# Reordering the top-16 search of two token tiles in a hybrid decoder step, with a different row cadence

## The chip, the cores and the metric

The kernel runs on one core of one Trainium2 chip. The metric is the device time of one execution in microseconds (us); of several runs the median is given. A smaller time is better. Five engines work side by side, each through its own instruction list in order: PE (TensorE, matrix products; its weight loads are shown apart as PEld), DVE (VectorE), ACT (ScalarE), POOL (GpSimd) and SP (SyncE, which only issues transfers here). They meet through semaphores, and 16 DMA engines move the data.

## The reference

One decoder layer is computed for 256 prompt tokens and 8 sample tokens that share all weights (D = 2048, everything float32):

```python
proj = x @ w_in
y_a = ssd_branch(...);  y_b = shortconv_branch(...)
mix = sigmoid(g_a) * (y_a @ w_branch_ssd) + sigmoid(g_b) * (y_b @ w_branch_sc)
x1 = layer_norm(ALPHA * x + mix @ w_out)
x2 = layer_norm(ALPHA * x1 + peer(x1))
y  = x2 + sigmoid(x2 @ ple_gate_w) * (p @ ple_proj_w)

def peer(x):                       # 8 heads, 16384 experts of one neuron each
    q = x @ w_q                    # per head two halves of 128
    t1, i1 = top_k(q[..., 0] @ keys1.T, 16);  t2, i2 = top_k(q[..., 1] @ keys2.T, 16)
    top, pos = top_k(all 256 sums t1 + t2, 16)
    idx = the expert numbers i1 * 128 + i2 at pos;  gate = softmax(top)
    hid = gelu(x . u_tab[idx]);  return sum over experts of gate * hid * v_tab[idx]
```

The change concerns `peer`, from the search over the scores to the products with the experts' rows.

## The kernel before

**Two ways to the experts.** For the first 208 prompt tokens (TD) the kernel works densely: it multiplies all 16384 experts' `u` rows with the tokens (the *u stage*: 128 blocks, one `pair_block` each), multiplies the result with a table of gates that is zero wherever an expert was not chosen, and multiplies that with all `v` rows (the *v stage*: 8 groups c of 16 blocks). The other 48 prompt tokens and the 8 samples (NSP = 56) are worked sparsely: for each of 56 columns a *row gather* (`get`, L1297, an indirect DMA on POOL's queue) brings 128 chosen rows of `uR`, 1 MB, and one DVE product over 128x2048 uses them; then the same with `vR`. That makes 112 row products, in three groups of 32, 16 and 8 columns, `u` before `v` in each (`sparse_experts`, L1289).

**What PE needs.** Every float32 weight is split into a rounded high part and the rest. A weight block of 1 MB is loaded by SP (L146) as two halves of 1024 columns; per half ACT writes `whi` (L158), DVE writes `wlo` (L159). Five pairs of `whi`/`wlo` exist in the u and v stages, so the split runs at most five halves ahead. A dense block is 15 + 1 products of 416 columns with `whi` (L293, the last one is L296) and 16 of 208 columns with `wlo` (L294).

**What sets the order.** The program is written out by Python, and the order on each engine is the order in which the code issues. After each half block `tick` raises a counter and lets background tasks (generators) issue work: each tick gives them a credit of 1.1 in these stages, and a yield of a number takes that credit, which stands for the DVE's time in us. A yield of ("w", n) waits n ticks. A task at the head of the list goes first. `Grid` keeps a task at a fixed step of ticks. Where the code needs a task's result before it can go on (`run_out`, or the loop after the u stage that waits for the last gates), it ticks with no block in between: then PE gets no instruction at that place.

**The selection.** `TT` names three tiles: tile 0 = tokens 128 to 255, tile 1 = the samples (64 rows, one per sample and head), tile 2 = tokens 0 to 127. `head_topk(h)` takes a head's scores; `topk` (L1095 to L1100, five DVE operations) finds the 16 best of 128 for one tile and one half. When all eight heads are done for all tiles, `select_all` runs `select` for tile 0, 1 and 2 in turn. `send` writes the sparse tokens' indices and gates to memory. `gates` (L1260) builds, four tokens per 3 ticks, the one-hot factors on POOL, DVE and ACT, `g_mm` multiplies them on PE (L1286), and a block of 32 tokens goes out to the table `g_d` (2 MB, L1278). Tokens 128 to 207 (20 steps) come after tile 0's selection, tokens 0 to 127 (32 steps) after tile 2's.

**The turn from u to v.** When the last gates are out, `to_v` gives the selection's memory to the v stage's buffers (`vp`), starts `residual` (16 ACT copies into `acc`, L1503) and `prep(0)`: four pieces k, each loading gates `gl` and hidden values `al` (L1430, L1431, L1433, two buffers each, on POOL's queue), multiplying them on DVE (L1446, L1447) and splitting the result into `co` (L1457 on ACT, L1458 on DVE). All four pieces must have been issued before the first block of v is (`run_out`).

Of the kernel before, what the change touches and what calls it, by code (L numbers as in the profile page):

```python
# [10 lines left out]
F = mybir.dt.float32  # L11
# [12 lines left out]
TD = T - NSP  # L24
# [6 lines left out]
PH = 8  # L31
# [12 lines left out]
STEP = 4  # L44
# [7 lines left out]
def hybrid_step(ctx: ExitStack, tc: tile.TileContext, xT, pT, w_in, w_dt, w_bs, w_bc, w_o, w_q, w_pg, w_pp,  # L52
# [111 lines left out]
    tasks = []  # L164
    later = []
    clock = {"t": 0, "credit": 0.0, "in": False}
# [892 lines left out]
    TT = ((PT // 2, 128, PH), (PT, 64, 1), (0, 128, PH))  # L1059
# [5 lines left out]
    t2_stack = ExitStack()  # L1065
# [36 lines left out]
    def head_topk(h):  # L1102
        load_keys(h)
        yield ("w", 2)
        for s in range(2):
            ac.copy(zq[:, s, h, 8 * h:8 * h + 8], Q[2 * h + s][:, PT:T])
        yield ("w", 1)
        k = keys_sb.pop(h)
        ps2 = {}
        for t in (0, 2):  # L1110
            t0, n, _ = TT[t]
            ps = bank("scr")
            for s in range(2):
                te.matmul(ps[:n, s * 128:(s + 1) * 128], Q[2 * h + s][:, t0:t0 + n], k[:, s], start=True, stop=True)
            v = t2.tile([128, 2, 128], F, name="sv", tag="sv", bufs=3)
            ac.copy(v[:n].rearrange("p s k -> p (s k)"), ps[:n, 0:256])
            ps2[t] = v
            yield 0.1
        if h == 0:
            SC["ps"] = bank("scp")  # L1120
        for s in range(2):
            te.matmul(SC["ps"][:64, s * 128:(s + 1) * 128], zq[:, s, h], k[:, s],
                      start=(h == 0 and s == 0), stop=(h == PH - 1), skip_group_check=True)
        if h == PH - 1:
            v = t2.tile([128, 2, 128], F, name="sv", tag="sv", bufs=3)
            ac.copy(v[:64].rearrange("p s k -> p (s k)"), SC.pop("ps")[:64, 0:256])
            ps2[1] = v
        for t, v in sorted(ps2.items()):
            n = TT[t][1]
            for s in range(2):  # L1130
                hh = h if t != 1 else 0
                topk(v[:n, s], TV[t][s][:n, hh], TI[t][s][:n, hh], n)
                yield 1.1
        Q.pop(2 * h)
        Q.pop(2 * h + 1)
        DONE[h] = True

    def select(t, sel):

# [66 lines left out]
    def select_all():  # L1206
        while sum(h in DONE for h in range(PH)) < PH:
            yield ("w", 1)
        t2_stack.close()
        sp = P["sp"] = sp_stack.enter_context(tc.tile_pool(name="select", bufs=1))  # L1210
        P["oh"] = oh_stack.enter_context(tc.tile_pool(name="onehot", bufs=1))
        for t, (t0, n, nh) in enumerate(TT):
            sel = sp.tile([128, 3, nh * TOPK], F, name=f"sel{t}")
            yield from select(t, sel)
            if t < 2:
                send(sel, t, nh)
            if t == 1:
                spawn(sparse_experts(), True)
            if t != 1:
                nd = min(n, TD - t0)  # L1220
                yield ("w", 2)
                ps = bank("slt")
                for q in range(3):
                    te.transpose(ps[:, q * 128:q * 128 + n], sel[:n, q], ident[:n, :n])
                for q in range(3):
                    ac.copy(slot[q][:, t0:t0 + nd], ps[:, q * 128:q * 128 + nd])
                if t == 0:
                    tasks.insert(0, {"gen": gates(t0, nd), "wait": clock["t"] + 1})
        while "G" + str(PT // 2) not in DONE:
            yield ("w", 1)  # L1230
        yield from gates(0, PT // 2)
# [57 lines left out]
    def sparse_experts():  # L1289
# [64 lines left out]
        for i, (tab, k0, n, c) in enumerate(jobs):  # L1354
            ks = slice(k0, k0 + n)
            if tab is uR and c == k0:
                x1s = XR.pop(g)
            if tab is vR and c == k0 and g + 1 < len(GR):
                while g + 1 == len(GR) - 1 and "sent" not in DONE:
                    yield ("w", 1)  # L1360
                index(g + 1)
                spawn(replicate(g + 1))
            get(i + 1)
            yield grid(STEP - (i % (4 if vp else 2) == 0))
            t = rows.pop(i)
            if tab is uR:
                ve.scalar_tensor_tensor(t, t, 1.0, x1s, OP.mult, OP.mult, accum_out=shid[:, c:c + 1])  # L1367
                yield 2.4
                if c == k0 + n - 1:
                    yield ("w", 1)  # L1370
                    ac.activation(shid[:, ks], shid[:, ks], AF.Gelu)
                    ve.tensor_tensor(scf[:, ks], shid[:, ks], scf[:, ks], OP.mult)
                continue
            if c == k0:
                ve.tensor_scalar(x1s, t, scf[:, c:c + 1], None, OP.mult)
            else:
                ve.scalar_tensor_tensor(x1s, t, scf[:, c:c + 1], x1s, OP.mult, OP.add)  # L1377
            yield 2.4
            if c == k0 + n - 1:
                spawn(folded(g, x1s), True)  # L1380
                g += 1
# [318 lines left out]
```

## Time and profile before

| | |
|---|---|
| median of 3 runs | 2459.51 us (2458.3 to 2460.56) |
| the profiled execution, its own time | 2465.26 us |
| its span, first to last instruction | 2463.5 us |
| mean granted PE clock over the span | 0.997 |
| last matmul of the first and of the last u block (L296) starts at | 1057.5 and 1738.5 us |
| the same of the v stage | 1743.1 and 2351.2 us |
| first and last row product (L1367, L1377) | 1250.5 and 2296.1 us |
| last copy-out of one-hot gates issued (L1278) | 1641.84 us |

Times inside the trace are microseconds from the start of the span. A row of the table of windows gives the length of the window and each engine's busy time in it with its number of instructions, then the granted PE clock (1.00 is full), the share of the 16 DMA engines' time that was in use, and GB/s. A row of the waits gives the engine and line that waited, what it waited for, the total, how often, and the longest. A row of the timeline or of a chain gives start, duration, engine, line, operation and tiles, and in square brackets the idle time of the engine ahead of it with what ended it.

### The profile page before, as it was taken

The numbers are of one execution on the slowest core, as the hardware profiler recorded it, in microseconds if no ns is written. First come the engines' busy times: TensorE is split into PE (matmuls) and PEld (weight loads), VectorE is DVE, ScalarE is ACT, GpSimd is POOL, SyncE is SP. The second block draws the span as 40 slices with busy tenths as digits, with TensorE's granted clock in tenths as the row PEclk, the third lists the DMA queues.
The fourth block names the chain that finished last, engine by engine and source line by source line (L and its number), as shares of the span: only waits on it lengthen the run. The fifth ranks groups of instructions, "written<-read, shape, count | busy, mean of one in ns | idle before, by whom it ended". The sixth has DMA issues, their size and how long they took to land.

```text
span 2463.5 us, 47946 instructions
## 1 busy us (share of the span) xinstructions
PE 2418.6 (98%) x19049; PEld 2394.8 (97%) x19049; DVE 2008.5 (82%) x3192; ACT 1458.7 (59%) x2310; POOL 620.0 (25%) x720
## 2 busy tenths in 40 slices
PE   9999999999999999999999999999999999999989
PEld 9999999999999999998999999999999999999988
DVE  8788886566455578999998777779999989989987
ACT  6776664554444455654777878866544555444564
POOL 2232221000000010100346667632332223322210
PEclk9999999999999999999999999999999999999999
DMA  6687786555555555566779999999999999999654
GB/s 247 229 289 260 261 265 204 193 189 202 191 202 191 193 201 189 196 212 203 238 291 347 358 359 372 368 352 396 399 374 382 382 375 392 376 374 371 223 190 147
DMA packets 137104, 688.90 MB, mean 280 GB/s; under 512 B 15744, under 2 KB 53168, under 8 KB 63280
## 3 DMA queue, kind: packets, MB, share of 16 engines
q1 hardware_dynamic: 89168, 495.46, 56.3%
q0 software_dynamic: 28688, 158.69, 16.7%
q10 hardware_dynamic: 19024, 31.69, 3.5%
q8 instruction: 149, 2.44, 0.4%
q14 instruction: 75, 0.61, 0.1%
HBM read 646.32 MB, written 39.46 MB: 278 GB/s over the span
## 4 chain that ended last, share of the span: by engine, by line
PE 63%; DVE 15%; DMA 11%; ACT 5%; issue 5%; ACTq 0%; POOL 0%; DVEq 0%; SPq 0%; POOLq 0%
PE mm L255 14%; PE mm L257 14%; PE mm L256 14%; PE mm L293 11%; DVE wlo L159 7%; PE mm L294 6%; DMA w<-vP 5%; DMA w<-uT 4%; ACT whi L158 2%; DVE ug L1367 1%; PE gps L1286 1%; ACT o L1274 1%; PE mm L296 1%; DMA a_d<-as 1%; DMA g_d<-gs 1%
## 5 line engine op out<-in xcount | busy, mean ns | idle before, releaser
L159 DVE TENSOR_TENSOR wlo<-w,whi 128x1024 fp32r<-128x1024 f32 x916 | 1112.0, 1223 | 333.9 <-ACT whi L158 328.0
L158 ACT CAST whi<-w 128x1024 fp32r<-128x1024 f32 x916 | 943.1, 1044 | 629.8 <-DMA w<-vP 247.0
L293 PE MATMUL mm<-x,whi 128*128 128x416 f32 x1920 | 572.7, 365 | 4.1 <-ACT whi L158 4.1
L293 PE MATMUL mm<-co,whi 128*128 128x416 f32 x1920 | 561.8, 361 | 0.0
L255 PE MATMUL mm<-x,whi 128*128 128x264 f32 x1920 | 532.4, 277 | 0.0
L257 PE MATMUL mm<-x,wlo 128*128 128x264 f32 x1920 | 530.2, 276 | 0.5 <-DVE wlo L159 0.4
L256 PE MATMUL mm<-x,whi 128*128 128x264 f32 x1920 | 529.9, 276 | 0.0
L294 PE MATMUL mm<-x,wlo 128*128 128x208 f32 x2048 | 504.7, 257 | 16.2 <-DVE wlo L159 15.9
L294 PE MATMUL mm<-co,wlo 128*128 128x208 f32 x2048 | 500.8, 255 | 7.2 <-DVE wlo L159 7.2
L294 PEld LDWEIGHTS mm<-x,wlo 128*128 128x128 f32 x2048 | 392.8, 193 | 25.0 <-DVE wlo L159 24.4
L294 PEld LDWEIGHTS mm<-co,wlo 128*128 128x128 f32 x2048 | 390.7, 192 | 11.5 <-DVE wlo L159 11.4
L293 PEld LDWEIGHTS mm<-x,whi 128*128 128x128 f32 x1920 | 365.6, 190 | 5.8 <-ACT whi L158 4.6
L255 PEld LDWEIGHTS mm<-x,whi 128*128 128x128 f32 x1920 | 362.9, 189 | 1.4 <-issue 1.4
L257 PEld LDWEIGHTS mm<-x,wlo 128*128 128x128 f32 x1920 | 362.9, 189 | 1.1 <-DVE wlo L159 1.1
L293 PEld LDWEIGHTS mm<-co,whi 128*128 128x128 f32 x1920 | 363.3, 189 | 0.0
L256 PEld LDWEIGHTS mm<-x,whi 128*128 128x128 f32 x1920 | 362.9, 189 | 0.0
L1273 POOL TENSOR_SCALAR o<-iot,slot,slot 128x128 f32<-128x128 f32 x156 | 191.1, 1232 | 2.7 <-issue 0.9
L1297 POOL DMA_INDIRECT ug<-vR,sidx x56 | 106.9, 1908 | 270.4 <-DVE x1s L1377 228.8
L1297 POOL DMA_INDIRECT ug<-uR,sidx x56 | 93.0, 1660 | 264.2 <-DVE ug L1367 204.8
L1367 DVE SCALAR_TENSOR_TENSOR ug<-ug,x1s 128x2048 f32<-128x2048 f32 x56 | 127.8, 2282 | 2.2 <-DMA ug<-uR,sidx 2.2
L1377 DVE SCALAR_TENSOR_TENSOR x1s<-ug,scf,x1s 128x2048 f32<-128x2048 f32 x53 | 124.4, 2347 | 0.4 <-DMA ug<-vR,sidx 0.4
L893 POOL CAST r1h<-r1gbh 128x2 fp32r<-128x2 f32 x16 | 7.5, 468 | 439.9 <-DVE mxl L242 439.9
(364 smaller groups left out, 3939.9 us busy)
## 6 DMA issues: line engine op xcount, KB each, us to landing
w<-uT SPq DMA_DIRECT2D x128, 1024.0 KB
w<-vP SPq DMA_DIRECT2D x128, 1024.0 KB
w<-w_in SPq DMA_DIRECT2D x118, 1024.0 KB
w<-w_bc SPq DMA_DIRECT2D x16, 1024.0 KB
w<-w_bs SPq DMA_DIRECT2D x16, 1024.0 KB
w<-w_o SPq DMA_DIRECT2D x16, 1024.0 KB
w<-w_q SPq DMA_DIRECT2D x16, 1024.0 KB
w<-w_pg SPq DMA_DIRECT2D x16, 1024.0 KB
```

The costliest lines, as they stand in the source:

```text
L158: ac.copy(hi, w)
L159: ve.tensor_tensor(lo, w, hi.bitcast(F), OP.subtract)
L255: te.matmul(ps, wh, vh, start=(first and q == 0), stop=False)
L256: te.matmul(ps, wh, vl, start=False, stop=False)
L257: te.matmul(ps, wl, vh, start=False, stop=(last and q == n - 1))
L293: te.matmul(ps, hi[:, ws], both, start=(kb == 0), stop=False)
L294: te.matmul(ps[:, :TD], lo[:, ws], one, start=False, stop=False)
L296: te.matmul(ps, hi[:, ws], both, start=False, stop=True)
L1273: (gp if q < 3 else ve).tensor_scalar(o1[:, q], iot, slot[0][:, c], slot[2][:, c], OP.is_equal, OP.mult)
L1297: gp.indirect_dma_start(out=t, out_offset=None, in_=tab, in_offset=bass.IndirectOffsetOnAxis(ap=sidx[:, c:c + 1], axis=0))
L1367: ve.scalar_tensor_tensor(t, t, 1.0, x1s, OP.mult, OP.mult, accum_out=shid[:, c:c + 1])
L1377: ve.scalar_tensor_tensor(x1s, t, scf[:, c:c + 1], x1s, OP.mult, OP.add)
```

## The change

Four things are altered. The second-stage score tiles `sv` of tile 2 get eight buffers of their own and are kept. `head_topk` searches only tile 0 and, at the last head, the samples; tile 2's 16 searches are done in `select_all`, after tile 0's selection. `sparse_experts` is started after tile 0's selection instead of after the samples', and the one-hot gates of tokens 128 to 207 start after tile 2's searches. The row products' cadence goes from 3 and 4 ticks in turn to 3, 4, 4, 4 in the u stage, and from 3, 4, 4, 4 to 4 throughout in the v stage (`vp` is set from the turn on).

```diff
         for t in (0, 2):
...
-            v = t2.tile([128, 2, 128], F, name="sv", tag="sv", bufs=3)
+            v = t2.tile([128, 2, 128], F, name="sv", tag="sv" + str(t), bufs=2 if t == 0 else PH)
...
+        late_sv.append(ps2.pop(2))
         for t, v in sorted(ps2.items()):
-            n = TT[t][1]
-            for s in range(2):
-                hh = h if t != 1 else 0
-                topk(v[:n, s], TV[t][s][:n, hh], TI[t][s][:n, hh], n)
-                yield 1.1
+            yield from tile_topk(t, v, h if t != 1 else 0)
...
+    late_sv = []
+
+    def tile_topk(t, v, h):
+        n = TT[t][1]
+        for s in range(2):
+            topk(v[:n, s], TV[t][s][:n, h], TI[t][s][:n, h], n)
+            yield 1.1
...
-        t2_stack.close()
         sp = P["sp"] = sp_stack.enter_context(tc.tile_pool(name="select", bufs=1))
-        P["oh"] = oh_stack.enter_context(tc.tile_pool(name="onehot", bufs=1))
         for t, (t0, n, nh) in enumerate(TT):
+            if t == 1:
+                for h, v in enumerate(late_sv):
+                    yield from tile_topk(2, v, h)
+                t2_stack.close()
+                P["oh"] = oh_stack.enter_context(tc.tile_pool(name="onehot", bufs=1))
+                tasks.insert(0, {"gen": gates(TT[0][0], TD - TT[0][0]), "wait": clock["t"] + 1})
             sel = sp.tile([128, 3, nh * TOPK], F, name=f"sel{t}")
             yield from select(t, sel)
             if t < 2:
                 send(sel, t, nh)
-            if t == 1:
+            if t == 0:
                 spawn(sparse_experts(), True)
...
-                if t == 0:
-                    tasks.insert(0, {"gen": gates(t0, nd), "wait": clock["t"] + 1})
...
-            yield grid(STEP - (i % (4 if vp else 2) == 0))
+            yield grid(STEP - (not vp and i % 4 == 0))
```

Two places show how the lists move. The first is DVE's list where the row products begin. In the kernel before, the first one (L1367, on tile `ug`) stands among the last selection's operations (`big`, `sel`) and the one-hot factors (`o_`), after 35 of the 128 u blocks (an `as` row closes a block):

```order
L1192 TENSOR_TENSOR big<-big,idf 128x512
L159 TENSOR_TENSOR wlo_13259<-w,whi_13258 128x1024
L1367 SCALAR_TENSOR_TENSOR ug,shid<-ug,x1s 128x2048
L159 TENSOR_TENSOR wlo_97<-w,whi_93 128x1024
L1412 TENSOR_TENSOR as<-mm,as 128x208
L159 TENSOR_TENSOR wlo_95<-w,whi_92 128x1024
L1273 TENSOR_SCALAR o_15422<-iot,slot_13263,slot_13265 128x128
L1194 TENSOR_REDUCE sel_14971<-big 128x32
```

In the changed kernel it stands after 24 blocks, among tile 2's searches (`tv`, `ti`, `sw`):

```order
L159 TENSOR_TENSOR wlo_95<-w,whi_92 128x1024
L1419 TENSOR_TENSOR as<-mm,as 128x208
L1374 SCALAR_TENSOR_TENSOR ug,shid<-ug,x1s 128x2048
L159 TENSOR_TENSOR wlo_96<-w,whi_91 128x1024
L159 TENSOR_TENSOR wlo_94<-w,whi_90 128x1024
L1419 TENSOR_TENSOR as<-mm,as 128x208
L1095 MAX tv_12040<-sv 128x8
L1096 MAX_INDEX ti_12046<-tv_12040,sv 128x8
L1098 MATCH_REPLACE sw<-tv_12040,sv 128x128
L1099 MAX tv_12040<-sw 128x8
L1100 MAX_INDEX ti_12046<-tv_12040,sw 128x8
L159 TENSOR_TENSOR wlo_13271<-w,whi_13270 128x1024
```

What moved: the row products now come with the searches of tile 2, and 25 of them (11 before) stand ahead of the end of tile 2's selection, which falls in block 70 (54 before).

The second place is DVE's list at the end of the u stage. In the kernel before, the last blocks of u (`as` rows) and the first of v (`acc`) stand next to each other, with only weight splits and row products between, since all four pieces of `co` were issued blocks earlier:

```order
L1377 SCALAR_TENSOR_TENSOR x1s<-ug,scf,x1s 128x2048
L159 TENSOR_TENSOR wlo_13259<-w,whi_13258 128x1024
L1412 TENSOR_TENSOR as<-mm,as 128x208
L159 TENSOR_TENSOR wlo_97<-w,whi_93 128x1024
L159 TENSOR_TENSOR wlo_95<-w,whi_92 128x1024
L1482 SCALAR_TENSOR_TENSOR acc<-acc,mm 128x416
L159 TENSOR_TENSOR wlo_96<-w,whi_91 128x1024
```

In the changed kernel three of the four pieces (`al<-al,gl`, then `co<-al,co`) stand behind the last `as` row, with row products in between and no weight split:

```order
L1419 TENSOR_TENSOR as<-mm,as 128x208
L1453 TENSOR_TENSOR al<-al,gl 128x4x192
L1454 TENSOR_TENSOR al<-al,gl 128x4x16
L1465 TENSOR_TENSOR co<-al,co 128x8x104
L1384 SCALAR_TENSOR_TENSOR x1s<-ug,scf,x1s 128x2048
L1453 TENSOR_TENSOR al<-al,gl 128x4x192
L1454 TENSOR_TENSOR al<-al,gl 128x4x16
L1465 TENSOR_TENSOR co<-al,co 128x8x104
L1384 SCALAR_TENSOR_TENSOR x1s<-ug,scf,x1s 128x2048
L1453 TENSOR_TENSOR al<-al,gl 128x4x192
L1454 TENSOR_TENSOR al<-al,gl 128x4x16
L1465 TENSOR_TENSOR co<-al,co 128x8x104
```

What moved: the last one-hot step stands after 119 u blocks instead of 105, `to_v` runs when 5 blocks of u are left instead of 19, and the preparation of the first v group goes past the end of u. Counted in ticks (two a block), 17 ticks lie between the last u block and the first v block, in which PE is given no dense block; before there are none. By the first v block 60 row products stand ahead (53 before), and the last of the 112 stands at half 209 of the 256 of v (232 before).

More of the change, by code (lines that the diff above doesn't have):

```diff
@@ L1124, in head_topk @@
         if h == PH - 1:
-            v = t2.tile([128, 2, 128], F, name="sv", tag="sv", bufs=3)
+            v = t2.tile([128, 2, 128], F, name="sv", tag="sv0", bufs=2)
             ac.copy(v[:64].rearrange("p s k -> p (s k)"), SC.pop("ps")[:64, 0:256])
             ps2[1] = v
+        late_sv.append(ps2.pop(2))
         for t, v in sorted(ps2.items()):
-            n = TT[t][1]
-            for s in range(2):
-                hh = h if t != 1 else 0
-                topk(v[:n, s], TV[t][s][:n, hh], TI[t][s][:n, hh], n)
-                yield 1.1
+            yield from tile_topk(t, v, h if t != 1 else 0)
         Q.pop(2 * h)
```

## The prediction

> **What bounds the kernel now.** First the page: which engine fills the span.
>
> ```profile
> span 2463.5 us, 47946 instructions
> PE 2418.6 (98%) x19049; PEld 2394.8 (97%) x19049; DVE 2008.5 (82%) x3192; ACT 1458.7 (59%) x2310; POOL 620.0 (25%) x720
> ```
>
> PE is busy 98% of the span, and its work does not change, so only its idle time can move. The windows say where that lies (length; busy PE, PEld, DVE, ACT, POOL; clock; DMA share; GB/s).
>
> ```profile
> core 0: us, PE busy (x) PEld busy (x) DVE busy (x) ACT busy (x) POOL busy (x), PEclk, DMA share, GB/s
> ...
> 1057.00:1142.00 85.00, 85.00 (x594) 83.36 (x594) 81.75 (x273) 45.36 (x76) 1.61 (x3) 1.00 0.66 220
> 1142.00:1260.00 118.00, 108.56 (x745) 105.98 (x744) 109.94 (x268) 80.26 (x132) 29.06 (x32) 0.99 0.68 230
> 1260.00:1500.00 240.00, 230.42 (x1623) 225.22 (x1623) 193.02 (x235) 187.39 (x332) 153.30 (x112) 1.00 0.92 349
> ...
> 1645.00:1664.00 19.00, 14.97 (x88) 14.22 (x87) 6.23 (x8) 6.92 (x13) 5.23 (x7) 0.85 0.91 327
> ...
> 1743.00:2050.00 307.00, 303.45 (x2109) 300.75 (x2107) 287.08 (x296) 150.40 (x183) 96.67 (x84) 1.00 0.98 381
> ...
> 2290.00:2362.00 72.00, 64.38 (x445) 62.98 (x444) 70.56 (x118) 41.72 (x79) 18.90 (x40) 0.98 0.61 208
> ```
>
> Four places lose time: the first half of u, where DVE is almost full (109.94 of 118) while DMA is not; the turn to v at 1645; the v stage with DMA at 0.98; and its end, where DVE is full again. The waits of PE's weight loads price them: 1057 to 1600 first, then 1700 to 2340, then 2290 to 2362 (which share about 1.8 us).
>
> ```profile
> PEld mm L294 <- DVE wlo L159: 21.0, 24, 3.1
> PEld slt L1224 <- DVE sel L1203: 3.5, 2, 2.2
> ```
>
> ```profile
> PEld mm L294 <- DVE wlo L159: 10.2, 14, 1.8
> ```
>
> ```profile
> PEld mm L1563 <- DVE acc L1484: 5.1, 2, 3.9
> PEld mm L294 <- DVE wlo L159: 3.8, 3, 1.8
> ```
>
> So about 25 us in early u, 8 in v and 9 at the end are all that could be won there. A block that waits for nothing takes 4.61 us, from one L296 to the next:
>
> ```profile
> 1611.15 0.36 PE L296 MATMUL mm<-x,whi 128*128 128x416 f32 x1
> ...
> 1615.76 0.36 PE L296 MATMUL mm<-x,whi 128*128 128x416 f32 x1
> ```
>
> **The turn to v.** This part decides. The chain of waits and the timelines show what happens once the last one-hot block is issued:
>
> ```profile
> 1641.84 15.14 DMA g_d<-gs
> ```
>
> ```profile
> 1646.43 0.33 ACT L1411 COPY as<-mm 128x208 f32<-128x208 f32 x1 [1.36 <-PE mm L296]
> 1657.08 1.01 ACT L1503 COPY acc<-x 128x416 f32<-128x416 f32 x2 [10.32 <-DMA g_d<-gs]
> ```
>
> ```profile
> 1655.23 0.36 PE L296 MATMUL mm<-x,whi 128*128 128x416 f32 x1
> 1659.08 0.71 PE L293 MATMUL mm<-x,whi 128*128 128x416 f32 x1 [3.49 <-ACT whi L158]
> ```
>
> ```profile
> 1667.06 0.36 PE L296 MATMUL mm<-x,whi 128*128 128x416 f32 x1
> ```
>
> The copy-out takes 15.14 us. ACT's next instruction, a copy into `acc`, needs that memory and holds ACT 10.32 us; behind it stand the `whi` splits; PE finishes two blocks from what was split, stops, and its third ends 11.83 us after the second, 7.2 more than a clean one. The change keeps this stall and moves it from 19 blocks ahead of the end of u to 5 ahead.
>
> Call the moment when the copy-out has landed (1657.1 here) T. The third block after the hand-over ends at T + 10.0 (1667.06). Before, 16 blocks of u followed, time enough for `prep(0)`; now 2 follow, and PE is out of u at T + 10.0 + 2 x 4.6 = T + 19.2. `prep(0)` by then has one of its four pieces. Its prices:
>
> ```profile
> L1377 DVE SCALAR_TENSOR_TENSOR x1s<-ug,scf,x1s 128x2048 f32<-128x2048 f32 x42 | 98.5, 2346 | 0.4 <-DMA ug<-vR,sidx 0.4
> ...
> L1458 DVE TENSOR_TENSOR co<-al,co 128x832 fp32r<-128x832 f32 x32 | 32.6, 1018 | 0.6 <-ACT co L1457 0.6
> L1446 DVE TENSOR_TENSOR al<-al,gl 128x768 f32<-128x768 f32 x32 | 30.4, 950 | 1.5 <-DMA al<-a_d 1.5
> ...
> L1447 DVE TENSOR_TENSOR al<-al,gl 128x64 f32<-128x64 f32 x32 | 7.0, 219 | 0.0
> ```
>
> ```profile
> L1457 ACT CAST co<-al x32: 957/986/1005, 1673.3 to 2249.8; 128x832 fp32r<-128x832 f32 x32
> ...
> DMA to landing us min/median/max: 6.8/9.7/12.6
> ```
>
> ```profile
> DMA to landing us min/median/max: 7.4/10.0/14.4
> ```
>
> The first landing row is that of `al`, the second that of the row gathers. A piece costs 0.95 + 0.22 + 0.99 + 1.02 = 3.2 us once loaded, and a row product of 2.35 stands between pieces. Piece 2 (loaded long before) starts behind the last block's sum at T + 19.6; ACT has a Gelu and two copies ahead of its cast, so it ends near T + 24; a row product to 26.4. Piece 3 was loaded when piece 1 gave its `al` buffer back, near T + 17.5, so its data is there at T + 27 and it ends near T + 30.4; a row product to 32.8. Piece 4's load waits for piece 2's buffer, T + 24, lands 9.7 later at T + 33.7, and the piece ends near **T + 37**. PE works the first three quarters of v's first block meanwhile and ends that block at T + 37 + 1.2 = T + 38.2 instead of T + 19.2 + 4.6 = T + 23.8: **14.4 us lost**. Then two row products stand ahead of the next `wlo` on DVE. A gather needs the buffer of the product two before it (T + 26.4 and T + 32.8), POOL's issue and 10.0 us: data at about T + 38 and T + 44.5, products done at T + 47, `wlo` at T + 48, while PE wants it after two more halves, at T + 42.8: **5 us**. The clock: after the 3.5 us of idleness above the matmul took 0.71 us instead of 0.36; of those 7.2 us the idleness explains about 4, the slow clock and what followed it the rest. Here a part of the slow time falls where the block waits anyway: **1.5**. The term is +21, less 1 for overlap of the last two: **+20**. Bounds: with landings at their minima (6.8, 7.4) piece 4 ends near T + 33 and the rows cost nothing, +10; at their maxima, +30.
>
> The Trainium skill bears on this (TensorE: Matmul & The Clock Gate, Part 1): after an idle window of about 3.4 us the PE clock falls to half, and comes back after about 3.4 us of sustained work. The 0.71 us matmul agrees. By that rule each long hole adds about 1.7 us, an estimate from that page, and the sum would be the same to within 1 us, so nothing above rests on it; it does speak against a change that trades many short waits for one long hole.
>
> **Early u.** Tile 2's searches are not saved, only moved: 25 searches stand behind the first u block, 24 before. What comes in is row products: 25 instead of 11 until the last selection ends, and that end comes 16 blocks later.
>
> ```profile
> L159 DVE TENSOR_TENSOR wlo<-w,whi 128x1024 fp32r<-128x1024 f32 x266 | 319.3, 1220 | 54.6 <-ACT whi L158 53.9
> ...
> L1367 DVE SCALAR_TENSOR_TENSOR ug<-ug,x1s 128x2048 f32<-128x2048 f32 x24 | 54.8, 2282 | 0.0
> ...
> L1412 DVE TENSOR_TENSOR as<-mm,as 128x208 f32<-128x208 f32 x18 | 6.6, 368 | 0.0
> ...
> L1367 DVE DVE_READ_ACCUMULATOR ug<-ug,x1s 128x1 f32 x24 | 1.9, 81 | 0.0
> ```
>
> A block leaves DVE 4.60 - 2 x 1.22 - 0.37 = 1.79 us. Sixteen blocks give 28.6; fourteen row products take 14 x 2.36 = 33.0, and the extra search and one-hot operation about 2. DVE owes 6 us more at the end of its full stretch. Against that, more than half of the 25 us of waits lies after 1260 (240.00 less 225.22 of busy weight loads), where DVE is 80% busy and a row product merely meets a split; at a step of 3.75 ticks instead of 3.5 there are fewer. I take **+4**, bounds -8 (most of those waits gone) and +9.
>
> **The v stage.** The 8 us of waits go with a full DMA:
>
> ```profile
> ACT whi L158 <- DMA w<-vP: 247.0, 102, 6.6
> ```
>
> Those 247 us are mostly slack of five halves, but each PE wait starts there. In v 52 row products stand where 59 stood, at 4 ticks instead of 3.75, and end 23 halves earlier. I take **-3**, bounds 0 and -8. **The end.** The last products and their fold leave the stretch where DVE is 70.56 of 72 busy, but the norm's own sums and the last `acc` adds remain: **-4** of the 9, bounds 0 and -9. POOL's lists stay far from full (153.30 of 240 at most), and the later one-hot steps cost PE the same; at nothing, covered by PE's own work.
>
> **Sum.** +20 + 4 - 3 - 4 = +17. Against the profiled execution's own 2465.26 that is 2482.3; the median of the runs is 5.75 lower, so 2459.5 + 17 = **2476.5 us**.
>
> **Rivals.** (1) *Balanced*: landings at their minima because SP, with its three weight buffers full, leaves DMA free while PE stands still. Turn +10, early u 0, v -4, end -6: 2459.5. For it: DMA fell to 0.91 at 1645 to 1664. Against: the order still puts three pieces and four row products in one file. (2) *Faster*, by one mechanism: the row gathers, not DVE's sums, are behind PE's waits in u, v and the end, and the wider step clears them. That brings -8, -8 and -9, and with the turn at +10 gives -15, **2444.5**. It decides from the point where the relief exceeds the turn's price. For it: DMA at 0.98 and the 247 us. Against: PE's waits in v are only 8 us in 610. (3) *Deeper hole*: gathers and loads at their maxima queue on POOL, turn +30, early u +9, nothing back: 2498.5. (4) *The rows do not begin earlier or spread*, since something else holds them: then only the later gates count, early u 0, v 0, end 0, turn +20: 2479.5, inside the forecast's range. The lists speak against it.
>
> **Chances.** Forecast (2465 to 2492, with rival 4) 0.62; balanced 0.16; faster 0.12; deeper 0.10. A measurement of this kernel tells about 0.2%, 5 us, from no change. Faster by more than that 0.13, within it 0.15, slower 0.72. The range 2456 to 2492 leaves out rival 3 and most of rival 2.
>
> **What would show it.** A hole on PE between the last u and the first v block, with `co` (DVE) as what ended it, 10 to 20 us long, followed by a wait for `wlo` behind a row product; the copy-out's stall of about 7 us now some 5 blocks ahead of it; in early u, waits for `wlo` of 20 to 30 us that last to about block 70; in v and at its end fewer. Wrong if the hole is under 8 us, or if the waits in early u halve.

## The result and the profile after

| | before | after |
|---|---|---|
| median of 6 runs each | 2459.18 us (2458.30 to 2460.56) | 2480.61 us (2479.50 to 2482.64) |
| the profiled execution, its own time | 2465.26 us | 2482.64 us |
| its span | 2463.5 us | 2480.7 us |
| mean granted PE clock | 0.997 | 0.990 |
| last matmul of the first and of the last u block (L296) starts at | 1057.5 and 1738.5 us | 1060.7 and 1738.15 us |
| the same of the v stage | 1743.1 and 2351.2 us | 1766.61 and 2368.5 us |

The ratio on record is 1.0078 with an interval of 1.0065 to 1.0092 (the two medians alone give 1.0087): the changed kernel is slower, by less than 1%. The medians differ by 21.4 us, the two profiled executions by 17.4 us, since the profiled execution of before lay 5.75 above the first median of before and that of after only 2.0 above its own. A second profile of the kernel before (run `e5` below) took 2463.62 us, 19.0 less than after.

The head of the page and its slices, the same rows as were shown of before with two more:

```profile
span 2480.7 us, 47936 instructions
PE 2422.8 (98%) x19049; PEld 2401.1 (97%) x19049; DVE 2010.2 (81%) x3192; ACT 1461.7 (59%) x2310; POOL 640.5 (26%) x720
PE   9999999999999999999999999999699999999999
PEclk9999999999999999999999999999799999999999
```

The work is the same to within 5 us on PE and 2 us on DVE. One slice of forty has a digit under 9, for PE and for its clock: slice 29, from 1736 to 1798 us. That is the place between u and v. The windows of the changed kernel (length; busy PE, PEld, DVE, ACT, POOL; clock; DMA share; GB/s):

```profile
1145.00:1260.00 115.00, 108.54 (x731) 105.96 (x731) 107.33 (x251) 69.86 (x112) 34.51 (x27) 0.97 0.85 300
...
1726.00:1742.00 16.00, 9.39 (x51) 8.71 (x50) 11.26 (x13) 10.96 (x17) 8.47 (x10) 0.88 0.83 293
1742.00:1772.00 30.00, 14.91 (x61) 13.57 (x62) 21.37 (x19) 12.73 (x20) 8.85 (x9) 0.55 0.86 324
1800.00:2100.00 300.00, 299.51 (x2096) 299.17 (x2095) 280.63 (x292) 150.91 (x183) 90.95 (x81) 1.00 0.98 381
2307.00:2380.00 73.00, 68.24 (x467) 67.41 (x467) 70.69 (x120) 45.30 (x84) 19.43 (x44) 0.95 0.63 212
```

In 1742 to 1772 PE issues 61 matmuls in 30 us, at a mean clock of 0.55, where it issues about 210 at its usual pace (2096 in 300 us). None of the other windows shown lost as much. In v PE is busy all the time, 299.51 of 300, though DMA is as full as before, 0.98. The waits of PE's weight loads, first 1060 to 1600, then 1700 to 1800, then 1800 to 2362:

```profile
PEld mm L294 <- DVE wlo L159: 21.0, 25, 3.5
```

```profile
PEld mm L293 <- DVE co L1465: 16.3, 3, 6.7
PEld mm L294 <- DVE wlo L159: 3.9, 3, 1.6
PEld mm L293 <- issue: 3.6, 1, 3.6
PEld mm L293 <- ACT whi L158: 2.7, 1, 2.7
```

```profile
PEld mm L294 <- DVE wlo L159: 0.8, 1, 0.8
```

The first row is the same sum as before (21.0). The second group is new, and is led by three waits for `co`. The wait of 3.6 that the profile puts down to `issue` ends with the first piece of `co`: DVE writes it until 1741.73, and PE's first matmul of v starts at 1741.84.

```profile
1740.72 1.01 DVE L1465 TENSOR_TENSOR co<-al,co 128x832 fp32r<-128x832 f32 x1
```

So PE waited for all four pieces. The third group was 10.2 us before (over 1700 to 2340).

**A ledger by stage.** To compare kernels, what PE lost is worked out for each stretch of blocks: the time between two starts of L296, less 4.60 us for each block, less PE's other work there (a one-hot step 0.89 us, four transposes of a row product's operand 0.43, a group of eight fold matmuls 0.89, the products of a head 1.67, a transpose of the selection 0.15). "Turn" is blocks 107 to 136, u and v counted through; the tail is from the last L296 to the end of the span.

| us lost by PE | early u, 0-72 | 72-107 | turn, 107-136 | v, 136-239 | end of v, 239-255 | tail |
|---|---|---|---|---|---|---|
| before | 27.0 | 1.1 | 10.8 | 6.0 | 4.3 | 112.3 |
| before, second profile | 25.5 | 2.1 | 12.5 | 6.2 | 1.5 | 112.5 |
| after | 29.7 | 2.4 | 33.2 | 0.8 | 0.7 | 112.2 |

After less before is +2.7, +1.3, +22.4, -5.2, -3.6 and -0.1, in all +17.5. The first L296 of u comes 3.2 us later since the score products of two heads have moved ahead of it; u then needs 3.3 us less of them, which cancels.

### The profile page after: what moved, and what is told of

Read it like the earlier page. It is cut to its first block, busy times and chain, and to the rows that moved or that the text cites. A ratio compares the mean times of both kernels' runs of the same rounds, so it can differ in the third digit from the quotient of the medians.

```text
span 2480.7 us, 47936 instructions
## 1 busy us (share of the span) xinstructions
PE 2422.8 (98%) x19049; PEld 2401.1 (97%) x19049; DVE 2010.2 (81%) x3192; ACT 1461.7 (59%) x2310; POOL 640.5 (26%) x720
## 4 chain that ended last, share of the span: by engine, by line
PE 78%; DVE 12%; DMA 4%; issue 3%; ACT 2%; ACTq 0%; POOL 0%; DVEq 0%; SPq 0%; POOLq 0%
PE mm L293 20%; PE mm L255 14%; PE mm L257 14%; PE mm L256 14%; PE mm L294 10%; DVE wlo L159 5%; DMA w<-uT 1%; PE mm L296 1%; DVE ug L1374 1%; PE gps L1293 1%; DMA ug<-vR,sidx 1%; ACT whi L158 1%; DVE as L1419 1%; DMA g_d<-gs 1%; DMA al<-a_d 1%
## 5 line engine op out<-in xcount | busy, mean ns | idle before, releaser
L293 PE MATMUL mm<-co,whi 128*128 128x416 f32 x1920 | 566.5, 364 | 18.4 <-DVE co L1465 15.1
L293 PEld LDWEIGHTS mm<-co,whi 128*128 128x128 f32 x1920 | 365.9, 191 | 20.0 <-DVE co L1465 16.3
L1280 POOL TENSOR_SCALAR o<-iot,slot,slot 128x128 f32<-128x128 f32 x156 | 214.3, 1381 | 1.7
L1304 POOL DMA_INDIRECT ug<-uR,sidx x56 | 97.4, 1740 | 292.8 <-DVE ug L1374 248.2
L1304 POOL DMA_INDIRECT ug<-vR,sidx x56 | 99.7, 1780 | 256.5 <-DVE x1s L1384 201.3
```

The lines of the kernel that those rows point to most:

```text
L293: te.matmul(ps, hi[:, ws], both, start=(kb == 0), stop=False)
L1280: (gp if q < 3 else ve).tensor_scalar(o1[:, q], iot, slot[0][:, c], slot[2][:, c], OP.is_equal, OP.mult)
L1304: gp.indirect_dma_start(out=t, out_offset=None, in_=tab, in_offset=bass.IndirectOffsetOnAxis(ap=sidx[:, c:c + 1], axis=0))
```

## The experiments

Theories are named in each expectation as it was written. What is left out or added is only what the short diff shows; all kernels do the whole computation.

**1. The turn alone.** The kernel before, with the hand-over to v held back until 5 blocks of u are left, as in the changed kernel.

```diff
-        if nxt is None and "G0" in DONE and not later:
+        if nxt is None and e >= 122 and "G0" in DONE and not later:
```

> The kernel before, with nothing changed but the turn from u to v: it is held back until 5 blocks of u are left, as in the changed kernel. Theory A (the late turn is the price): a hole on PE ahead of v's first blocks of 18 to 25 us, 2474 to 2484 us in all, since the v stage gains 2 or 3 us from row products done in the hole. Rival B (the price is DVE's load from row products among the searches, the late turn only shows where it comes out): within 5 us of the kernel before, 2455 to 2464.

Measured: 2475.79 us (2474.96 to 2477.89) against 2463.69 for the kernel before in the same set; 1.0055 [1.0042, 1.0069]. PE's waits at 1690 to 1790:

```profile
PEld mm L293 <- DVE co L1458: 14.4, 3, 5.9
PEld mm L293 <- issue: 6.4, 1, 6.4
```

The same three waits for `co` appear though neither searches, rows nor cadence were touched. The turn loses 29.3 us, 18.5 more than in the first profile of before. v and its end get 6.0 of that back (3.6 and 0.7): empty ticks in the hole let row products run ahead while PE stands.

**2. The one-hot gates faster.** The changed kernel, its last 32 steps at 2 and 3 ticks in turn instead of 3, so that they end earlier.

```diff
-            yield grid(3)
+            yield grid(3 if t0 else 2 + (tt // 4) % 2)
```

> The changed kernel, with the one-hot steps of tokens 0 to 127 at 2 and 3 ticks in turn instead of 3, so that they end 18 ticks (9 blocks) earlier and the turn comes when 11 blocks of u are left instead of 5. Theory A: PE's losses at the turn fall from 33 us to between 12 and 18, so 2460 to 2467 us. Rival B: the turn's hole moves into early u or v and the time stays at 2476 to 2484. Rival C (ACT cannot do a one-hot step every 2.5 ticks): the whi splits come late and blocks 72 to 112 lose over 10 us, 2470 or more.

Measured: 2473.57 us (2471.03 to 2475.16); 1.0042 [1.0029, 1.0056]. The turn falls from 33.2 to 14.9 as expected, but blocks 72 to 107, through which the faster steps run, lose 10.1 instead of 2.4. The waits of PE's weight loads at 1442 to 1680, then the windows at 1440 to 1660, of this kernel first and of the changed kernel behind it:

```profile
PEld mm L294 <- DVE wlo L159: 7.2, 4, 4.6
```

```profile
1440.00:1660.00 220.00, 213.75 (x1519) 212.20 (x1519) 161.73 (x181) 185.33 (x338) 156.64 (x116) 0.98 0.90 337
```

```profile
1440.00:1660.00 220.00, 218.10 (x1560) 216.58 (x1560) 171.97 (x189) 183.75 (x325) 145.90 (x107) 1.00 0.94 357
```

So 18 us were won at the turn, 8 lost where the gates were hurried and 4 in v (4.8 instead of 0.8). The time came 7 us nearer to before, not the 13 to 20 expected. The two numbers of rival C came true (10.1 us in blocks 72 to 112, and over 2470), but not its cause: at 1442 to 1680 DVE waited 52.5 us for `whi`, and 52.2 in the changed kernel. 7.0 of the 10.1 us fell in one block (88), where DVE waited for the first gather of `vR` rows, which was issued behind 11 us of one-hot work in POOL's list:

```profile
1525.69 2.35 DVE L1384 SCALAR_TENSOR_TENSOR x1s<-ug,scf,x1s 128x2048 f32<-128x2048 f32 x1 [8.24 <-DMA ug<-vR,sidx]
```

**3. The changed kernel with the old cadence of rows.**

```diff
-            yield grid(STEP - (not vp and i % 4 == 0))
+            yield grid(STEP - (i % (4 if vp else 2) == 0))
```

> The changed kernel with the old cadence of row products (3 and 4 ticks in turn in u; 3, 4, 4, 4 in v). The row products take more of the credit, the last selection ends 8 ticks later and one block of u is left at the turn instead of 5. Theory A: the hole grows by about 4 blocks less what is already idle in it, +8 to +14, 2488 to 2495 us. Rival D (the wider cadence is what relieves v and early u, the turn costs the same): +3 to +6, 2483 to 2487, with the losses in v back at 8 us or more.

Measured: 2499.51 us (2493.68 to 2505.61); 1.0145 [1.0127, 1.0164], 19 above the changed kernel, more than either theory had. Rows that come more densely push the gates back until one block of u is left at the turn. The turn then costs 42.4 us, and v 7.7. One row of the waits at 1700 to 1800 holds it:

```profile
PEld yS L1345 <- DVE x1s L1384: 37.8, 1, 37.8
```

PE's next instruction there is the fold (L1345) of a finished group of row products; with no dense block issued, it is put down to that. By the ledger 9.2 us of it are the turn, 6.9 v and 4.4 blocks 72 to 107, less 1.1 in early u. The wider cadence in u therefore *helped* the changed kernel: it lets the gates end earlier.

**4. The new cadence alone**, in the kernel before (the same line, the other way).

> The kernel before with the wider cadence alone. The turn stays where it was (19 blocks left), so no hole there by theory A; early u and v lose 2 to 6 us less. But the last row product comes at v's half 250 of 256 and its fold is done only after v's last block, so PE waits there for the norm: +8 to +15. In all 2460 to 2470 us. Rival D (the cadence relieves DMA everywhere): 2450 to 2456, with no hole at the end of v.

Measured: 2485.20 us (2479.75 to 2487.80); 1.0094 [1.0079, 1.0109]. The tail grows by 13 (125.4) since the last row product now stands at half 250 of 256 and its fold comes behind v. That was expected; but v, which was to gain, loses 13.6 and its end 8.7. Early u loses only 18.1. So the wider cadence does not by itself relieve v. Experiments 11 and 12 come back to this.

**5. The kernel before again**, for a second profile.

> The kernel before, profiled a second time. Its first profiled execution took 5.75 us more than its median, and the late-turn kernel, with the same instructions up to block 109 of u, lost 4 us less in blocks 39 to 72. If those 4 us are a matter of the execution, the second profile shows 7 to 11 us of losses there instead of 13, and the rise in early u against the changed kernel is 6 to 8 us, not 3. If it shows 12 to 14 again, the 3 us stand.

Measured: 2463.62 us; its ledger is in the table above. The turn, v and tail agree with the first profile within 2 us, the end of v within 2.8. Blocks 39 to 72 lost 11.7 us here and 13.2 in the first, but 8.8, 7.6 and 8.9 in experiments 1, 7 and 9, whose instructions there are the same. The second profile lies between the two expectations, but the spread over five executions settles it: a difference of 3 or 4 us in early u is not to be trusted.

**6. Row products held through the hole**, in the changed kernel: from the last block of u to the first of v no row is fetched or used.

```diff
+            while P.get("hold"):
+                grid.t += 1
+                yield ("w", 1)
             get(i + 1)
...
+    P["hold"] = True
     while len(ACC) < KB:
...
         run_out(nxt)
+        P["hold"] = False
```

> The changed kernel with the row products (their gathers too) held from the end of u until the first v block is given out, and then going on at their step. Theory A with its second half (row products and gathers stand among the pieces and ahead of the next weight split): the losses at the turn fall from 33 us to between 21 and 27, so 6 to 9 us less than the changed kernel, at 2471 to 2476. Rival E (the pieces' loads alone set the hole): under 3 us of change, 2477 to 2482.

Measured: 2480.44 us (2477.24 to 2483.84); 1.0069 [1.0052, 1.0086]. The turn fell to 27.3, so the rows in the hole cost 5.9 us; but v lost 10.3 instead of 0.8 and took it back. The waits for `co` stayed (14.6 us, the longest 7.5, where 16.3 and 6.7 stood), and in v DVE waited once for 8.51 us for a load of `al`, behind which PE stood (the timelines of DVE and of PE):

```profile
PEld mm L293 <- DVE co L1468: 14.6, 3, 7.5
```

```profile
2083.74 0.96 DVE L1456 TENSOR_TENSOR al<-al,gl 128x768 f32<-128x768 f32 x1 [8.51 <-DMA al<-a_d]
```

```profile
2086.03 0.54 PE L294 MATMUL mm<-co,wlo 128*128 128x208 f32 x1 [3.66 <-DVE wlo L159]
```

**7. The old stall taken out.** In the kernel before, the copies into `acc` that hold ACT for 10.32 us wait 8 ticks longer, and `prep(0)` waits 8 instead of 4 ticks for its first load.

```diff
-                yield ("w", 4)
+                yield ("w", 4 if c else 8)
...
-        spawn(residual())
+        spawn(residual())["wait"] = clock["t"] + 8
```

> The kernel before with the copies into acc and the first piece's products issued 8 ticks after the turn instead of at once, so that ACT and DVE do not stand behind the copy-out. Theory A says that the stall there is ACT's: the 7 us hole at block 112 goes, losses of blocks 107 to 136 fall from 11 us to 3 to 5, and the kernel is 5 to 8 us faster than before. Rival F (the copy-out takes DMA from the weights, and those are late anyway): within 2 us of before.

Measured: 2463.95 us (2460.52 to 2468.38); 1.0012 [1.0001, 1.0023], not faster. ACT is free, but the load of `gl`, which waits for the same copy-out, now holds POOL's list, the row gathers stand behind it, and DVE waits for one of them (the waits of POOL, then of DVE, at 1630 to 1720). POOL's row names an ACT copy that ended at about the same time; by the semaphores in the trace the copy-out landed at 1655.06, and the load went out at 1655.68:

```profile
POOL gl L1430 <- ACT as L1411: 19.0, 1, 19.0
```

```profile
DVE x1s L1377 <- DMA ug<-vR,sidx: 8.1, 1, 8.1
```

A wait for memory was moved from ACT's list to POOL's, and PE's hole went with it: PE waited 8.2 us two blocks later.

**8. The row products begun early, alone**: the kernel before, with only this line.

```diff
-            if t == 1:
+            if t == 0:
                 spawn(sparse_experts(), True)
```

> The kernel before with the row products begun after the first tile's selection, and nothing else of the change: searches, one-hot steps and cadence as before. The last selection ends 13 ticks later (not 32), 13 blocks of u are left at the turn. Theory A: 13 blocks cover the copy-out and nearly all pieces, so the turn loses 11 to 16 us instead of 11, and the row products end before the last v group, which gives 3 to 4 back: within 4 us of before. Rival B (row products among the selection cost DVE the time): early u loses 5 or more, and the kernel is 5 to 10 us slower than before.

Measured: 2475.77 us (2471.32 to 2482.03); 1.0054 [1.0037, 1.0071], where no change was expected. Early u is not worse (24.6). The gates end 6 blocks later, with 13 blocks of u left, and the turn loses 20.9 with 6 ticks in which PE gets no block; blocks 72 to 107 lose 8.7, 5.0 of it in one wait behind a row product whose gather was late (DVE's waits at 1530 to 1560):

```profile
DVE x1s L1377 <- DMA ug<-vR,sidx: 10.2, 1, 10.2
```

The profiled execution was the slowest of the six, 6.3 us above their median, so its ledger is on the high side. Still, this one line makes the kernel 14.9 us slower than the kernel before in the same set, more than either theory had.

**9 and 10. Copies and preparation both put off**, by 8 and 7 ticks in the kernel before (9), and by 4 in the changed one (10), so that no list should stand behind the copy-out.

```diff
         t = spawn(prep(0), True)
-        spawn(residual())
+        t["wait"] = clock["t"] + 7
+        spawn(residual())["wait"] = clock["t"] + 8
```

> The kernel before with all of the turn's work held: the first loads of gl and al 7 ticks and the copies into acc 8 ticks later, so that neither ACT, DVE nor POOL (whose row gathers stand behind those loads) waits for the copy-out of the last one-hot block. Theory A, mended: whichever list holds the first instruction that needs the copy-out is what stalls; with none, the losses of blocks 107 to 136 fall from 11 to 12 us to between 3 and 6 us, and the kernel takes 5 to 8 us less than before, 2451 to 2457. Rival F (the copy-out takes DMA from the weights): within 2 us of before.

> The changed kernel with the loads and the copies of the turn held 4 ticks. Theory A: the stall of the copy-out is part of the hole that the pieces make, since only 5 blocks of u are left; PE ends u 4 to 7 us earlier and waits as much longer, and the time stays within 3 us of the changed kernel, 2477 to 2484. Rival: the two add up, and 4 to 7 us go, 2473 to 2477.

Measured: 2461.27 us (2454.97 to 2464.12) for 9, 1.000 [0.999, 1.001]; 2479.71 us (2474.08 to 2482.80) for 10, 1.0073 [1.0058, 1.0089]. In the profile of 9 ACT no longer waits for the copy-out, POOL still does for 4.0 us, and PE's hole is gone (blocks 107 to 121 lose 2.8 us, and no wait of PE's weight loads at 1630 to 1720 is over 1.1):

```profile
PEld mm L294 <- DVE wlo L159: 5.1, 7, 1.1
```

That execution was its fastest, though, and the medians are equal: whether the gain is real and given back elsewhere stays open. In 10 the turn loses 32.8 against 33.2, but the run does not settle its question: 4 ticks were too few, and ACT's list and POOL's (12.7 us) still waited for the copy-out (ACT's waits at 1700 to 1740):

```profile
ACT acc L1510 <- DMA g_d<-gs: 7.9, 1, 7.9
```

PE's stall only moved one block on (block 127 lost 5.8 us). The nearest look at a late turn without the stall is experiment 1, where the copy-out had landed at 1658.4, long before the turn at about 1705: from the end of block 122 to the end of the first v block it took 52.5 us, against 56.9 in the changed kernel and 59.3 in 10. So the stall may cost some 4 us of its own; no run shows this in the changed kernel.

**11 and 12. The phase of the row products in v.** A group of v has 32 ticks, a multiple of the new cadence of 4, so the rows come at the same ticks of every group, and so do the loads of `al` and `gl`, which share POOL's list with the row gathers. In experiments 4 and 6 the rows are used at ticks 2, 6, 10, 15, 18, 22, 27, 30 in every full group; in the changed kernel so too at first, but after the third group at 0, 4, 9, 12, 16, 21, 24, 28, because a boundary between groups of columns adds a few ticks. Kernel 11 is experiment 4 with one extra gap of 2 ticks at row product 50; kernel 12 is the changed kernel with the same gap at row product 82, which puts the old phase back.

```diff
             get(i + 1)
+            grid.t += 2 * (i == 50)
             yield grid(STEP - (not vp and i % 4 == 0))
```

> The kernel before with the new cadence alone, as in an earlier run, but with one extra gap of 2 ticks at row product 50, the first full group of v: a group of v has 32 ticks, so a cadence of 4 puts the row products at the same ticks of every group (2, 6, 10, 15, 18, 22, 27, 30 in that run; 0, 4, 9, 12, 16, 21, 24, 28 in this one). Theory P (what v loses under a cadence of 4 is set by that phase: in the first one the loads of al stand behind row gathers in POOL's list, DVE waited 27.0 us for them in six waits, and PE lost 13.6 us in blocks 136 to 239): DVE's waits for al fall to 0 to 8 us, the loss in 136 to 239 to 0.5 to 4, the end of v still loses 5 to 10 with the rows running to its end, and the time is 8 to 12 below the 2485.2 of that run: 2473 to 2478. Rival Q (the loss comes from the number of row products that are still to be done in v, whatever their phase): loss 10 to 15 as there, time 2480 to 2489.

> The changed kernel with one extra gap of 2 ticks at row product 82, so that from the fourth group of v on its row products stay at ticks 2, 6, 10, 15, 18, 22, 27, 30 of each group, where the changed kernel has gone over to 0, 4, 9, 12, 16, 21, 24, 28 by then. Nothing is left out or added. Theory P (the phase sets it): DVE's waits for al between 1790 and 2300, 5.4 us in the changed kernel, rise to 12 to 25, PE's loss in blocks 136 to 239, 0.8 there, rises to 4 to 9, and the time is 3 to 8 above the changed kernel: 2483 to 2489. Rival Q (the number of row products sets it): loss 0.5 to 2, time within 2 us of 2480.6.

Measured: 11 took 2467.82 us (2464.03 to 2477.11), 1.0027 [1.0010, 1.0044], 17.4 below experiment 4 (15.2, each taken against the kernel before in its own set) and 5 below the range expected; 12 took 2487.19 us (2485.98 to 2496.78), 1.0095 [1.0065, 1.0124], 6.6 above the changed kernel (4.2, each against its own set), as expected. DVE's waits for `al` at 1790 to 2300 were none in 11; in 4 and in 12 they were

```profile
DVE al L1446 <- DMA al<-a_d: 27.0, 6, 7.3
```

```profile
DVE al L1454 <- DMA al<-a_d: 21.5, 5, 7.2
```

and PE's loss in blocks 136 to 239 was 3.9 in 11 (13.6 in experiment 4) and 14.4 in 12 (0.8 in the changed kernel; 4 to 9 expected). But the gap at row product 82 acts from block 174 on, and 7.9 of 12's 14.4 us fell ahead of that block, where its instructions are still those of the changed kernel; its profiled execution was the slowest, 9.6 us above its median. From block 174 on 12 lost 6.5 us and the changed kernel 0.0. DVE's waits for `al` there, at 1990 to 2300, were none in the changed kernel, and in 12

```profile
DVE al L1454 <- DMA al<-a_d: 13.2, 3, 7.2
```

POOL's timeline shows how: in experiment 4 the first load of a group stands right behind a row gather that waited for its buffer,

```profile
1886.73 1.68 POOL L1297 DMA_INDIRECT ug<-uR,sidx  x1 [4.93 <-DVE ug L1367]
1888.41 0.90 POOL L1430 DMA_DIRECT2D gl<-g_d  x1
```

and in 11 that load goes out ahead of that gather:

```profile
1879.36 0.90 POOL L1431 DMA_DIRECT2D gl<-g_d  x1
1880.23 0.63 POOL L1432 DMA_DIRECT2D gl<-gr_d  x1
1880.80 0.59 POOL L1434 DMA_DIRECT2D al<-a_d  x1
1884.31 1.73 POOL L1297 DMA_INDIRECT ug<-uR,sidx  x1 [2.92 <-DVE ug L1368]
```

Two ticks of phase, with nothing else changed, thus move the median by 15 to 17 us in the one pair. (The profiled executions of 4 and 11 differ by 12.5, of which v and its end are 9.7 and 2.6.) In the other pair the 4 to 7 us are not clear of noise by the times alone: the interval of 12 overlaps that of the changed kernel, 1.0065 to 1.0092.

Blocks 174 to 239 of all the kernels with a cadence of 4 in v show the phase best. In the first phase 4, 6 and 12 lose 6.6, 7.3 and 6.5 us there; in the second the changed kernel, 10 and 11 lose 0.0, 0.7 and 2.8; in a third one (1, 6, 9, 14, 17, 21, 26, 29) experiment 2 loses 4.8. Ahead of block 174 it is less clear: the first phase lost 7.0, 3.0 and 7.9 in 4, 6 and 12, but 0.8 in the changed kernel, with the same instructions as 12. So the first phase lets the loads collide, and how often it costs PE time differs between executions. The old cadence drifts through all phases and loses 2.9 to 10.8 in all of v in the six kernels that have it.

The ledger of all experiments:

| us lost by PE | early u | 72-107 | turn | v | end of v | tail |
|---|---|---|---|---|---|---|
| 1 late turn | 22.6 | 2.5 | 29.3 | 3.6 | 0.7 | 112.5 |
| 2 fast gates | 27.1 | 10.1 | 14.9 | 4.8 | 0.7 | 112.1 |
| 3 old cadence | 28.6 | 6.8 | 42.4 | 7.7 | 0.6 | 112.5 |
| 4 cadence alone | 18.1 | 1.9 | 10.8 | 13.6 | 8.7 | 125.4 |
| 6 rows held | 27.2 | 2.6 | 27.3 | 10.3 | 0.6 | 112.2 |
| 7 late copies | 22.7 | 1.0 | 15.3 | 2.9 | 2.0 | 112.6 |
| 8 rows early alone | 24.6 | 8.7 | 20.9 | 10.8 | 0.7 | 112.7 |
| 9 turn later, before | 22.7 | 1.0 | 9.2 | 4.7 | 1.3 | 112.5 |
| 10 turn later, after | 27.2 | 3.6 | 32.8 | 0.7 | 0.7 | 112.0 |
| 11 cadence shifted | 19.3 | 0.9 | 8.6 | 3.9 | 6.1 | 128.5 |
| 12 after, phase kept | 27.6 | 6.7 | 30.5 | 14.4 | 0.7 | 112.6 |

None of them beats the kernel before.

## Why the prediction was right, point by point

**The sum.** Forecast +17 on the profiled execution: it was +17.4, and +19.0 against the second profile. The median came out 4.1 us above the forecast: the 5.75 us by which the first profiled execution exceeded its median were taken off in full. The changed kernel's runs spread over only 3.1 us, and its profile lay 2.0 above its median. In the later sets the medians of the kernel before were 2460.85 to 2463.69, nearer to that profile.

**The turn, +20 forecast, +22.4 measured (+20.7 against the second profile).** The mechanism is the one forecast: experiment 1 makes it alone in the kernel before, and experiment 2 takes 18 of it away. Its parts were sized less well. T, the landing of the copy-out, is 1726.6 here. The chain of waits and ACT's timeline show the same stall:

```profile
1710.10 16.41 DMA g_d<-gs
```

```profile
1726.61 1.01 ACT L1510 COPY acc<-x 128x416 f32<-128x416 f32 x2 [9.57 <-DMA g_d<-gs]
```

PE's and DVE's timelines show what follows:

```profile
1738.15 0.36 PE L296 MATMUL mm<-x,whi 128*128 128x416 f32 x1
```

```profile
1741.84 0.69 PE L293 MATMUL mm<-co,whi 128*128 128x416 f32 x1 [3.33 <-issue]
1750.47 0.71 PE L293 MATMUL mm<-co,whi 128*128 128x416 f32 x1 [6.09 <-DVE co L1465]
1759.32 0.71 PE L293 MATMUL mm<-co,whi 128*128 128x416 f32 x1 [6.28 <-DVE co L1465]
1764.60 0.71 PE L293 MATMUL mm<-co,whi 128*128 128x416 f32 x1 [2.72 <-DVE co L1465]
1766.61 0.59 PE L296 MATMUL mm<-co,whi 128*128 128x416 f32 x1
1772.25 0.36 PE L296 MATMUL mm<-co,whi 128*128 128x416 f32 x1
```

```profile
1749.39 1.02 DVE L1465 TENSOR_TENSOR co<-al,co 128x832 fp32r<-128x832 f32 x1 [1.84 <-ACT co L1464]
1750.33 2.35 DVE L1384 SCALAR_TENSOR_TENSOR x1s<-ug,scf,x1s 128x2048 f32<-128x2048 f32 x1
1756.15 0.96 DVE L1453 TENSOR_TENSOR al<-al,gl 128x768 f32<-128x768 f32 x1 [3.47 <-DMA al<-a_d]
1758.23 1.03 DVE L1465 TENSOR_TENSOR co<-al,co 128x832 fp32r<-128x832 f32 x1 [0.99 <-ACT co L1464]
1763.52 1.03 DVE L1465 TENSOR_TENSOR co<-al,co 128x832 fp32r<-128x832 f32 x1 [0.99 <-ACT co L1464]
1764.46 2.34 DVE L1384 SCALAR_TENSOR_TENSOR x1s<-ug,scf,x1s 128x2048 f32<-128x2048 f32 x1
1768.14 2.35 DVE L1384 SCALAR_TENSOR_TENSOR x1s<-ug,scf,x1s 128x2048 f32<-128x2048 f32 x1 [1.34 <-DMA ug<-vR,sidx]
```

- *PE leaves u at T + 19.2*: it left at 1738.15 + 0.36, T + 12. This is the step that failed, for two reasons. The blocks were miscounted by one: in both kernels the stalled block is the fourth after the hand-over, not the third. Before, it is block 112, with 15 blocks of u behind it and not 16; after, it is block 126, with one behind it and not two (4.6 us). And the stall was milder: block 126 lost 4.4 us, not 7.2, and ended at T + 5.9 instead of T + 10.0. The block behind it lost 1.0.
- *The pieces*: forecast T + 24, 30.4 and 37; measured T + 23.8 (1750.4), T + 32.7 (1759.3) and T + 38 (1764.55). The first piece was not ready when PE left u, as the forecast had it, but at T + 15.1. The landing of `al` took 14.0 us for piece 3 where its median of 9.7 had been used.
- *The first v block, 14.4 us lost*: 1766.61 - 1738.15 is 28.46, less 4.60 is 23.9. PE left u 7 us earlier than forecast and met the same pieces; so what is missing in the stall stands in the hole, and the end of the block is off by only 2 us (T + 40 for T + 38.2). That the two trade fully is argued from these times; experiment 10 left the stall in place and cannot show it.
- *Then 5 us for a `wlo` behind two row products*: block 129 lost 1.0. Those rows stand there, at 1764.46 and 1768.14, but DVE waited only 1.34 us for the second one's gather; it landed after 6.25 us, not 10.0. The forecast took the median, and less than the least of before (7.4) came true.
- *The clock, 1.5*: about 2. The clock was 0.55 through the hole, where PE waited for `co` anyway. But after the last of these waits, from 1764.60 to the end of block 129 at 1772.25, PE waits for nothing; matmuls take 0.59 us instead of 0.36 until 1768.6, and the stretch takes 7.65 us where a clean one takes 5.47 (4.60 and three steps of 0.29). The 1.0 us of block 129 is this, not a wait for `wlo`.

The Trainium skill (TensorE: Matmul & The Clock Gate, Part 1) has the clock back after about 3.4 us of sustained work. The trace agrees: in the hole no burst of matmuls was that long, and the clock stayed down until v ran steadily.

The total came nearer than its parts, which is partly luck: the hole was 9.5 us larger than forecast (23.9 for 14.4), against a milder stall (2.8 less) and the `wlo` behind the rows, forecast at 5, which never came.

**Early u, +4 forecast, +2.7 or +4.2 measured**: right as a number, its reason not shown. The row products were to fill DVE. But early rows alone did not cost anything there (experiment 8: 24.6), the wider cadence alone lost 18.1 and 19.3 us (4 and 11) where the old one lost 22.6 to 27.0, and executions with the same instructions differ by about 4 us. What costs the changed kernel its 27 to 30 us there stays open: no run moves tile 2's searches alone.

**v, -3 forecast, -5.2 measured; the end, -4 forecast, -3.6 or -0.8 measured.** Signs and sizes hold, but the reason given for v, fewer row products at a wider step, fell: the wider step alone makes v worse in one phase (experiment 4, 13.6) and not clearly better in the other (11, 3.9), and the changed kernel falls into a good phase halfway. From block 174 on, that is the gain: 0.0 lost for 3.1 and 3.6 before, and 12 takes it away. Ahead of it 0.8 was lost for 3.0 and 2.7, which the phase does not explain. The number for v came true by luck. For the end the reason stands: where the rows are done ahead of it (1, 2, 3, 6, 8, 10, 12) it loses 0.6 to 0.7; where they run to the end of v (4, 11), 8.7 and 6.1.

**POOL and the moved one-hot steps, at nothing**: blocks 72 to 107 lost 1.3 more. It holds at 3 ticks a step; at 2.5 a gather behind POOL's one-hot work came late (experiment 2).

**The rivals.** *Balanced* and *faster* needed a cheap turn and relief in v: the relief came, the cheap turn did not. The time of *deeper hole* (2498.5) is near what the old cadence makes of it (experiment 3, 2499.5), but there the gates came later, and not the landings. *The rows do not begin earlier* gave 2479.5, the nearest of all, but its condition was not met: the row products ran from 1188.5 to 2261.6 us, where they ran from 1250.5 to 2296.1 before.

## What to carry to other kernels

Before background work is reordered, look for the point at which a stage cannot begin until the last of that work is out, and count how many blocks are left to cover the preparation behind it: here 6 blocks less of cover cost about 9 us at the turn (experiment 8), 14 less about 20. Where several tasks share an in-order list at a cadence, compare the cadence with the period of the stage: if it divides it, the same collision comes back in every round, and here two phases differed by about 10 us of PE's time over v (experiments 4 and 11); try the phases before judging the cadence. Taking one wait for memory out of one list can move it to the next list that needs the same memory (experiment 7); with both lists held back the hole went, though the median did not move (experiment 9).

## What the runs showed of the hardware that was not expected

Short bursts did not bring the PE clock back: in the trace's clock records half clock begins at 1741.4 us and lasts 27.3 us, through three bursts of matmuls of about 2.5 us each (from a start to the next start less its wait, as in 1759.32 - 6.28 - 1750.47) with waits of 2.7 to 6.3 us between them, until 4 us after the last wait; in experiment 3 it lasted 41.0 us.

What a transfer takes is not told by its size: in the changed kernel the same 1 MB row gather landed after 5.6 to 13.1 us, and the same load of `al` after 4.7 to 14.0 us, within 80 us of one execution. What makes the difference no run here shows.
